# The first gate product of a DeltaNet/attention block, emitted with the last step of the scan

## The chip, the cores and the metric

The kernel runs on one core of one Trainium2 chip. The metric is the device time of one execution in microseconds (us), given as the median of several runs of the same program. A run is also taken with the hardware profiler; its rows are what this document reads. TensorE is called PE in them, VectorE DVE, ScalarE ACT, GpSimd POOL, and SP is the queue engine that issues most DMA transfers (ACT issues the rest).

## The reference, cut to what matters

One transformer-like layer on 1024 tokens of width 1024, all float32. The input projection's columns feed two groups of heads: a gated DeltaNet group (4 heads of 128, chunkwise with a state carried through the sequence) and a latent attention group (8 heads). Their outputs are joined, projected, normalised and added; a squared-ReLU MLP follows. The part that the change touches is the end of the DeltaNet group:

```python
    _, o = lax.scan(step, state0, xs)
...
    o = gated_delta_rule(q, k, v, beta, log_a)
    g = jax.nn.silu(gate.astype(jnp.float32)).reshape(bsz, s, GDN_HEADS, GDN_HEAD_DIM)
    o = rms_norm(o, out_norm) * g
...
        mixed = jnp.concatenate([o_gdn.astype(x.dtype), o_mla.astype(x.dtype)], axis=-1) @ w_out[l]
```

`gate` is one more 512-column slice of the input projection `h @ w_in`. So the gate of a head needs the normalised input and that head's 1024x128 block of the weight, and not the scan; only its product with the normalised scan output `o` does.

## The kernel before, in words

Every float32 matrix product that must be exact is done as three matmuls of split operands (`mm3`, lines 206 to 209): a high and a low part of each side. `stream` (L201) loads a 512 KB weight block into a `raw` buffer (three exist), and `split` (L196) makes the pair: a cast on ACT (L198, tile `whi`) and a subtraction on DVE (L199, tile `wlo`); three such pairs exist too. All such loads, and those of `load_head` and `gate`, go through `load_chained` (L182), which ties each to the one before: on SP they are issued in the order in which the program emitted them.

The work runs in stages. First come the normalisation, the projections and the preparation of the DeltaNet chunks. These are interleaved by `Weave`, a planner with costs written by hand. Then `scan()` (L861) goes through 8 chunks of 128 tokens and two more passes that drain it. It has its own PSUM pool, `psS`: four banks `pq` for the short products, two `po` for the outputs, two `ps`. In its pass c the outputs of chunk c-1 are finished (`outputs`, matmuls L916 and L917 into `ps_O`), normalised (`out_norm`, L921) and, one pass later, turned around by four transposes on PE, scaled on ACT and written to the DRAM tensor `d_go` (`out_rows`, L932, lines 937 to 939). `out_norm` is a chain: four squares with a sum on ACT (L927), one small operation on DVE (L928), a square root on ACT (L155), five small operations on DVE and the scaling of the whole tile (L930). Only then can the four transposes of that chunk start.

After the scan a new PSUM pool, `psB`, serves the attention. `units` lists 64 score blocks, a head and a block of 128 query rows each; for each the loop from L1185 on emits scores, softmax, transposes of the probabilities and the product with the values. Between them it emits pieces of `background()` (L1130): eight gate products `gate(h, half)` (L1092; a head and half of the tokens each, 24 matmuls in four pieces), then the DeltaNet part of the output projection. Ten pieces are emitted before the first score block, then about one with each.

A gate product needs PSUM bank `ou`, of which there is one; a Tanh on ACT (L1103), a combination on DVE that frees the bank (L1104), a product with the normalised scan output on POOL (L1105), and a write of the result to `d_gate` (L1106). Its scan output comes back from DRAM as tile `go` (two buffers), a load that must wait until the rows of `d_go` are written. `w_gate` holds the split weights of the four heads' gates: blocks 12 and 13 of the input weight are requested in passes 2 and 4 of the scan, block 14 after the first gate product and block 15 after the third.

A scheduler sets the order of instructions on each engine when the program is built, from the order of emission, the dependences and its own model of time; each engine then runs its list in that order, and an instruction that waits holds up all behind it on its engine.

Of the kernel before, what the change touches and what calls it, by code (L numbers as in the profile page):

```python
# [8 lines left out]
F32 = mybir.dt.float32  # L9
# [8 lines left out]
P = 128  # L18
# [86 lines left out]
def build(tc, a, out):  # L105
# [756 lines left out]
    def scan():  # L862
# [4 lines left out]
        for c in range(NT + 2):  # L867
            s = slice(c * P, (c + 1) * P)
            if c < NT:
                if c % 2 == 0:  # L870
                    yield f"load{c // 2}"
                if c in (2, 4):
                    w_gate.append(stream(a["w_qkvg"][11 + c // 2]))
# [29 lines left out]
            if 1 <= c <= NT:  # L903
                out_norm(c - 1)
            if c >= 2:
                out_rows(c - 2)
                if c % 2:
                    free("b", 3)
            yield step(5.0, 4.0, 3.0, lat=None)

    def outputs(c, heads):
# [57 lines left out]
    def load_values(h, lo):  # L969
        v = raw_tile()[:, :HALF].rearrange("p (b c) -> p b c", c=64)  # L970
        load_chained(v, d_v[:, :, h])
        e = h % 2
        V[h] = vt = vtile(f"V{h}").rearrange("p (b c) -> p b c", c=P)
        pair_of((vt[:, :, 64 * e : 64 * e + 64], vt[:, :, 64 - 64 * e : P - 64 * e]), v, lo)

    def filler():
# [114 lines left out]

    def gate(h, half):  # L1092
        s = slice(half * HALF, (half + 1) * HALF)
        o = lp.tile([P, HALF], F32, name="go", tag="go", bufs=2)
        load_chained(o, d_go[h, :, s])
        ps = psum("ps_gate", "ou")
        for k in range(KT):
            mm3(ps, cut(w_gate[h], slice(None), slice(k * P, (k + 1) * P)), h_cols(half, k), k == 0, k == KT - 1)
            if k % 2 and k < KT - 1:
                yield  # L1100

        g = lp.tile([P, HALF], F32, name="gate", tag="gate", bufs=2)
        nc.scalar.activation(g, ps, AF.Tanh, scale=0.5)  # L1103
        nc.vector.scalar_tensor_tensor(g, g, 1.0, ps, op0=ALU.add, op1=ALU.mult)  # L1104
        nc.gpsimd.tensor_tensor(g, g, o, op=ALU.mult)  # L1105
        nc.scalar.dma_start(d_gate[h, :, s], g)  # L1106
        yield

    def load_tokens(dst, src, j):
# [20 lines left out]
    def background():  # L1130
        for h, half in ((0, 0), (0, 1), (1, 0), (1, 1), (2, 0), (3, 0)):
            yield from gate(h, half)
            if h < 2 and half == 0:
                w_gate.append(stream(a["w_qkvg"][14 + h]))
            if (h, half) == (1, 1):
# [566 lines left out]
```

## Time and profile before

| what | value |
|---|---|
| median of 3 runs | 1280.64 us (1278.71 to 1283.99) |
| profiled execution | 1280.36 us |
| its span in the profile | 1278.6 us |
| PE busy | 1222.9 us (96% of the span) |
| DVE, ACT, POOL busy | 903.9, 651.9, 163.4 us |
| mean granted clock of PE | 0.985 |

The span lies inside the time of the execution; the 1.8 us between them are around the program's first and last instruction. In the rows of a timeline stand the start in us, the length in us, engine, line, operation, what it writes and reads, and in brackets how long the engine was idle before it and what ended that. A clock of 1.00 is PE's full speed.

### The profile page before, as it was taken

The page shows a single profiled execution, that of the slowest core. Times are in us where ns is not written, and L with a number is a line of the kernel's source. Part 1 is how long each engine was busy: PE and PEld are TensorE (multiplying, and loading weights), DVE is VectorE, ACT ScalarE, POOL GpSimd, SP SyncE. Part 2 cuts the span into 40 slices and gives each one's busy share as a digit, 9 for nine tenths or more (in the row PEclk, how much of TensorE's full clock was granted, in tenths as well). Part 3 has the DMA queues.
Part 4 walks back from the last instruction along what each step waited for, and adds up shares of the span by engine and source line. Part 5 has one row for each costly group of instructions (what it writes and reads, how often), then busy time and mean ns, then how long its engine had stood idle before and what let it go on. Part 6 is the DMA issues. An engine that isn't in the chain of part 4 may idle for free.

```text
span 1278.6 us, 17685 instructions
## 1 busy us (share of the span) xinstructions
PE 1222.9 (96%) x6224; PEld 1035.5 (81%) x6224; DVE 903.9 (71%) x1779; ACT 651.9 (51%) x1189; POOL 163.4 (13%) x152
## 2 busy tenths in 40 slices
PE   7999999999889999999898999999999999999995
PEld 6978888899778878887686888888887888888884
DVE  7678889546556785686976777677656786776744
ACT  6567643425645786774555544444445433344431
POOL 1011011220044553430000000000000000011021
PEclk9999999999989999999898999999999999999998
DMA  5114535736342511124444455455449984555902
GB/s 233 47 61 149 186 119 194 214 86 176 97 139 87 161 50 31 42 67 148 157 164 158 148 201 196 162 206 188 174 154 410 365 295 148 193 165 202 343 19 98
DMA packets 111217, 205.71 MB, mean 161 GB/s; under 512 B 33557, under 2 KB 51989, under 8 KB 111130
## 3 DMA queue, kind: packets, MB, share of 16 engines
q1 hardware_dynamic: 94848, 176.09, 41.1%
q10 hardware_dynamic: 16282, 28.50, 6.0%
q8 instruction: 49, 0.80, 0.3%
q14 instruction: 38, 0.31, 0.1%
HBM read 143.07 MB, written 61.49 MB: 160 GB/s over the span
## 4 chain that ended last, share of the span: by engine, by line
PE 60%; DVE 5%; DMA 3%; ACT 2%; issue 1%; POOL 1%; SPq 0%; DVEq 0%; ACTq 0%; POOLq 0%
PE ps_up L207 8%; PE ps_up L209 8%; PE ps_up L208 8%; PE ps_dn L208 8%; PE ps_dn L209 8%; PE ps_dn L207 8%; PE ps_PT L1061 2%; PE ps_out L207 2%; PE ps_out L208 1%; PE ps_out L209 1%; PE ps_o L1080 1%; PE ps_sc L207 1%; PE ps_o L1079 1%; PE ps_sc L208 1%; PE ps_sc L209 1%
## 5 line engine op out<-in xcount | busy, mean ns | idle before, releaser
L1573 POOL TENSOR_TENSOR rows<-rows,gpost 128x512 f32<-128x512 f32 x16 | 23.9, 1512 | 654.8 <-ACT junk L1570 654.8
L209 PE MATMUL ps_proj<-hThi,wlo 128*128 128x512 f32 x192 | 75.1, 395 | 1.2 <-DVE wlo L199 1.2
L207 PE MATMUL ps_proj<-hThi,whi 128*128 128x512 f32 x192 | 76.0, 396 | 0.0
L208 PE MATMUL ps_proj<-hTlo,whi 128*128 128x512 f32 x192 | 76.0, 396 | 0.0
L1065 DVE TENSOR_TENSOR PTlo<-ps_PT,PThi 128x512 fp32r<-128x512 f32 (+2 forms) x96 | 52.0, 550 | 20.0 <-ACT PThi L1064 19.3
L1064 ACT CAST PThi<-ps_PT 128x512 fp32r<-128x512 f32 (+2 forms) x96 | 45.4, 481 | 29.7 <-PE ps_PT L1061 28.1
L1505 DVE TENSOR_TENSOR dlo<-draw,dhi 128x1024 fp32r<-128x1024 f32 x35 | 44.7, 1301 | 22.0 <-ACT dhi L1504 21.9
L208 PE MATMUL ps_dn<-dlo,dhi 128*128 128x512 f32 x144 | 56.0, 389 | 0.0
L209 PE MATMUL ps_dn<-dhi,dlo 128*128 128x512 f32 x144 | 56.0, 389 | 0.0
L207 PE MATMUL ps_dn<-dhi 128*128 128x512 f32 x144 | 55.5, 389 | 0.0
L1325 ACT CAST whi<-raw 128x1024 fp32r<-128x1024 f32 (+1 forms) x29 | 26.3, 906 | 54.7 <-PE ps_up L208 48.9
L1035 ACT ACTIVATE Pt<-ps_sc,nm 128x896 f32<-128x896 f32 (+3 forms) x64 | 48.0, 749 | 11.8 <-DVE nm L1033 7.6
L1504 ACT CAST dhi<-draw 128x1024 fp32r<-128x1024 f32 x35 | 36.1, 1048 | 34.1 <-issue 13.8
L1061 PE MATMUL ps_PT<-ident,Pt 128*128 128x128 f32 x288 | 46.6, 276 | 2.4 <-DVE PTlo L1065 1.2
L1033 DVE TENSOR_REDUCE nm<-ps_sc 128x1 f32<-128x896 f32 (+3 forms) x64 | 47.8, 750 | 1.2
L1040 POOL TENSOR_TENSOR Pt<-Pt,rs 128x128 f32<-128x128 f32 (+4 forms) x40 | 35.4, 885 | 89.1 <-DVE rs L1038 65.1
L199 DVE TENSOR_TENSOR wlo<-raw,whi 128x1024 fp32r<-128x1024 f32 (+1 forms) x27 | 33.7, 1251 | 17.5 <-ACT whi L198 14.9
L1079 PE MATMUL ps_o<-PThi,V 128*128 128x256 f32 (+1 forms) x160 | 41.2, 280 | 3.2 <-DVE o L1086 1.4
L209 PEld LDWEIGHTS ps_proj<-hThi,wlo 128*128 128x128 f32 x192 | 36.1, 188 | 9.2 <-DVE wlo L199 1.7
L208 PEld LDWEIGHTS ps_proj<-hTlo,whi 128*128 128x128 f32 x192 | 36.1, 188 | 7.4 <-issue 0.5
L207 PEld LDWEIGHTS ps_proj<-hThi,whi 128*128 128x128 f32 x192 | 36.1, 188 | 7.4 <-issue 0.5
L1080 PE MATMUL ps_o<-PTlo,V 128*128 128x256 f32 (+1 forms) x160 | 41.2, 300 | 0.0
(589 smaller groups left out, 3969.6 us busy)
## 6 DMA issues: line engine op xcount, KB each, us to landing
draw<-in_w_down_dram SPq DMA_DIRECT2D x47, 512.0 KB
draw<-d_act SPq DMA_DIRECT2D x41, 512.0 KB
raw<-in_w_up_dram SPq DMA_DIRECT2D x40, 512.0 KB
raw<-in_w_down_dram SPq DMA_DIRECT2D x17, 512.0 KB
raw<-in_w_qkvg_dram SPq DMA_DIRECT2D x16, 512.0 KB
d_act<-c SPq DMA_DIRECT2D x16, 512.0 KB
d_act<-s SPq DMA_DIRECT2D x16, 512.0 KB
raw<-d_act SPq DMA_DIRECT2D x15, 512.0 KB
```

The lines of the kernel that those rows point to most:

```text
L207: mm(ps, lhs[0], rhs[0], start=start, stop=False, **kw)
L208: mm(ps, lhs[0], rhs[1], start=False, stop=False, **kw)
L209: mm(ps, lhs[1], rhs[0], start=False, stop=stop, **kw)
L1033: nc.vector.tensor_reduce(nm, ps[:, :npc, :w], axis=AX.XY, op=ALU.max, negate=True)
L1035: nc.scalar.activation(Pt[:, :n].rearrange("p (i w) -> p i w", i=npc), ps[:, :npc, :w], AF.Exp, bias=nm, scale=1.0, accum_out=sm)
L1061: transpose(ps[:, j * P : (j + 1) * P], Pt[:, b * P : (b + 1) * P], ident)
L1064: nc.scalar.copy(hi[:, :n, cs], ps3)
L1065: nc.vector.tensor_sub(lo[:, :n, cs], ps3, hi[:, :n, cs].bitcast(F32))
L1079: mm(ps[:, cs], V[h][:, b], hi[:, cs], start=(b == 0), stop=False)
L1080: mm(ps[:, cs], V[h][:, b], lo[:, cs], start=False, stop=(b == nb - 1))
L1504: nc.scalar.copy(hi, raw)
L1505: nc.vector.tensor_tensor(lo, raw, hi.bitcast(F32), op=ALU.subtract)
```

## The change

`gate` moves up, next to the scan, and can take its PSUM bank and its two tiles from other pools. The last pass of the scan (c = 9) starts `gate(0, 0)` with a bank of the scan's `pq` set and with tiles `hf` of the scan's memory, and emits three of its four pieces; the fourth follows after the pass. `background()` therefore has seven gate products left and begins with `gate(0, 1)`. The third gate's weight, block 14, is requested in pass 6 of the scan, as 12 and 13 are in passes 2 and 4; block 15 is still requested after `gate(1, 0)`. Lines of the scan after the new code are six higher than before: L917 is now L923, L927 is L933, L937 is L943, L939 is L945; the gate's Tanh is L994, its DVE and POOL operations L995 and L996, its write L997.

```diff
@@ -869,7 +869,7 @@
             if c < NT:
                 if c % 2 == 0:
                     yield f"load{c // 2}"
-                if c in (2, 4):
+                if c in (2, 4, 6):
                     w_gate.append(stream(a["w_qkvg"][11 + c // 2]))
                 kb = block(c)[0]
                 if c > 0:
@@ -902,11 +902,17 @@
                         )
             if 1 <= c <= NT:
                 out_norm(c - 1)
+            if c == NT + 1:
+
+                g = gate(0, 0, "pq", half_tile)
+                for _ in range(3):
+                    next(g)
             if c >= 2:
                 out_rows(c - 2)
                 if c % 2:
                     free("b", 3)
             yield step(5.0, 4.0, 3.0, lat=None)
+        next(g)
 
     def outputs(c, heads):
         _, pb, qb = block(c)
@@ -972,6 +978,24 @@
         e = h % 2
         V[h] = vt = vtile(f"V{h}").rearrange("p (b c) -> p b c", c=P)
         pair_of((vt[:, :, 64 * e : 64 * e + 64], vt[:, :, 64 - 64 * e : P - 64 * e]), v, lo)
+
+    def gate(h, half, tag="ou", tile=None):
+        s = slice(half * HALF, (half + 1) * HALF)
+        tile = tile or (lambda name: lp.tile([P, HALF], F32, name=name, tag=name, bufs=2))
+        o = tile("go")
+        load_chained(o, d_go[h, :, s])
+        ps = psum("ps_gate", tag)
+        for k in range(KT):
+            mm3(ps, cut(w_gate[h], slice(None), slice(k * P, (k + 1) * P)), h_cols(half, k), k == 0, k == KT - 1)
+            if k % 2 and k < KT - 1:
+                yield
+
+        g = tile("gate")
+        nc.scalar.activation(g, ps, AF.Tanh, scale=0.5)
+        nc.vector.scalar_tensor_tensor(g, g, 1.0, ps, op0=ALU.add, op1=ALU.mult)
+        nc.gpsimd.tensor_tensor(g, g, o, op=ALU.mult)
+        nc.scalar.dma_start(d_gate[h, :, s], g)
+        yield
 
     def filler():
         yield "v1"
@@ -1089,23 +1113,6 @@
                 mixT[p] = mtile(f"mixhi{p}"), mtile(f"mixlo{p}")
             pair_of(cut(mixT[p], slice(None), hs), oT[p][:, hs], nc.gpsimd)
 
-    def gate(h, half):
-        s = slice(half * HALF, (half + 1) * HALF)
-        o = lp.tile([P, HALF], F32, name="go", tag="go", bufs=2)
-        load_chained(o, d_go[h, :, s])
-        ps = psum("ps_gate", "ou")
-        for k in range(KT):
-            mm3(ps, cut(w_gate[h], slice(None), slice(k * P, (k + 1) * P)), h_cols(half, k), k == 0, k == KT - 1)
-            if k % 2 and k < KT - 1:
-                yield
-
-        g = lp.tile([P, HALF], F32, name="gate", tag="gate", bufs=2)
-        nc.scalar.activation(g, ps, AF.Tanh, scale=0.5)
-        nc.vector.scalar_tensor_tensor(g, g, 1.0, ps, op0=ALU.add, op1=ALU.mult)
-        nc.gpsimd.tensor_tensor(g, g, o, op=ALU.mult)
-        nc.scalar.dma_start(d_gate[h, :, s], g)
-        yield
-
     def load_tokens(dst, src, j):
         load_chained(dst.rearrange("p (h t) -> p h t", h=GH), src[:, :, 256 * j : 256 * (j + 1)].rearrange("h p t -> p h t"))
 
@@ -1128,10 +1135,10 @@
         return mtile("whi4"), mtile("wlo4")
 
     def background():
-        for h, half in ((0, 0), (0, 1), (1, 0), (1, 1), (2, 0), (3, 0)):
+        for h, half in ((0, 1), (1, 0), (1, 1), (2, 0), (3, 0)):
             yield from gate(h, half)
-            if h < 2 and half == 0:
-                w_gate.append(stream(a["w_qkvg"][14 + h]))
+            if (h, half) == (1, 0):
+                w_gate.append(stream(a["w_qkvg"][15]))
             if (h, half) == (1, 1):
                 w = [[stream(a["w_out"][0, 0])], []]
         load_gates((0,), raw_tile)
```

The next pieces show, word for word, where instructions stand in the lists of three engines.

ACT, end of the scan, before. `oj` is the square of a chunk's outputs (L927, "x2" two heads), `qb` the scaled transposes, `ro_t` the square root; `kT`, `qT` and `V` are the operands of the first attention head.

```order
L927 ACTIVATE oj,so<-ps_O 128x128 x2
L938 ACTIVATE qb_3247<-ps_onT,cols 128x512
L927 ACTIVATE oj,so<-ps_O 128x128
L939 DMA d_go<-qb_3247 128x4x128
L927 ACTIVATE oj,so<-ps_O 128x128
L155 ACTIVATE ro_t<-so 128x4
L943 CAST kT_3601<-raw 96x1024
L943 CAST qT_3603<-raw 96x1024
L943 CAST V_3617<-raw 128x8x64
L938 ACTIVATE qb_3247<-ps_onT,cols 128x512
L939 DMA d_go<-qb_3247 128x4x128
L198 CAST whi<-raw 128x1024
```

The same place on ACT after the change:

```order
L944 ACTIVATE qb_3247<-ps_onT,cols 128x512
L933 ACTIVATE oj,so<-ps_O 128x128
L994 ACT_TABLE_LOAD
L994 ACTIVATE gate<-ps_gate 128x512
L945 DMA d_go<-qb_3247 128x4x128
L933 ACTIVATE oj,so<-ps_O 128x128
L155 ACT_TABLE_LOAD
L155 ACTIVATE ro_t<-so 128x4
L997 DMA d_gate<-gate 128x512
L949 CAST kT_3639<-raw 96x1024
L944 ACTIVATE qb_3247<-ps_onT,cols 128x512
L949 CAST qT_3641<-raw 96x1024
```

The gate's Tanh now stands between the third and the fourth square of the last chunk, with a load of ACT's function table ahead of it and another one ahead of the square root. Before, the first Tanh stood behind the cast of a weight (`whi`), after the last chunk was done. Behind the rows shown come, after the change, the cast of `V`, the write of the last chunk to `d_go`, the cast of block 15's weight, a third table load and the Tanh of `gate(0, 1)`.

PE at the same place, before. `ps_O` with `vtok_2528` and `vtok_2957` are the last two heads' outputs of the last chunk, `ps_onT` the transposes, "x8" those of the last two chunks.

```order
L886 MATMUL ps_s_3510<-vtok_2957,Z_2773 128x128
L917 MATMUL ps_O<-vtok_2189,pb_3244 128x128
L916 MATMUL ps_O<-kb_3241,qb_3247 128x128
L917 MATMUL ps_O<-vtok_2528,pb_3244 128x128
L916 MATMUL ps_O<-kb_3241,qb_3247 128x128
L917 MATMUL ps_O<-vtok_2957,pb_3244 128x128
L937 MATMUL ps_onT<-ident,pb_3244 128x128 x8
L207 MATMUL ps_gate<-hThi_142,whi 128x512
```

PE after the change, from the last five of the eighteen gate matmuls that now stand ahead of the last two heads' outputs (two more stand ahead of `vtok_2189`):

```order
L207 MATMUL ps_gate<-hThi_144,whi 128x512
L208 MATMUL ps_gate<-hTlo_145,whi 128x512
L923 MATMUL ps_O<-vtok_2528,pb_3244 128x128
L922 MATMUL ps_O<-kb_3241,qb_3247 128x128
L923 MATMUL ps_O<-vtok_2957,pb_3244 128x128
L943 MATMUL ps_onT<-ident,pb_3244 128x128 x4
L209 MATMUL ps_gate<-hThi_144,wlo 128x512
L207 MATMUL ps_gate<-hThi_144,whi 128x512
L208 MATMUL ps_gate<-hTlo_145,whi 128x512
L209 MATMUL ps_gate<-hThi_144,wlo 128x512
L943 MATMUL ps_onT<-ident,pb_3244 128x128 x4
L207 MATMUL ps_gate<-hThi_146,whi 128x512
```

So 20 of the 24 matmuls of `gate(0, 0)` stand ahead of the last chunk's last outputs, four between the two groups of transposes, and `gate(0, 1)` (`hThi_146`) follows behind the last transposes. Behind it come the first two score blocks and then `gate(1, 0)`, which needs the one bank `ou` that `gate(0, 1)` holds.

SP behind the scan's own loads, before:

```order
L183 DMA go<-d_go 128x512
L183 DMA raw<-in_w_qkvg_dram 128x1024
L183 DMA go<-d_go 128x512 x2
L183 DMA raw<-d_k 64x1024
L183 DMA raw<-d_kr 32x1024
L183 DMA raw<-d_q 64x1024
L183 DMA raw<-d_r 32x1024
L183 DMA raw<-in_w_qkvg_dram 128x1024
```

SP after the change:

```order
L183 DMA go<-d_go 128x512
L183 DMA raw<-d_k 64x1024
L183 DMA raw<-d_kr 32x1024
L183 DMA raw<-d_q 64x1024
L183 DMA raw<-d_r 32x1024
L183 DMA raw<-d_v 128x8x64
L183 DMA go<-d_go 128x512 x2
L183 DMA raw<-in_w_qkvg_dram 128x1024
L183 DMA go<-d_go 128x512
L183 DMA raw<-d_k 64x1024
```

The first head's five loads, which before stood far ahead among the loads of the preparation, now stand behind the first `go`; block 14's load has gone up to their former place (with its cast and subtraction); and the next weight load, now block 15, stands behind two loads of `go`, the first of which reads the last chunk's rows of `d_go`. Before, the next weight load (block 14) stood ahead of that one.

## The prediction

> **What bounds the kernel now.** I read the page first, then the windows around the end of the scan, then the timelines of PE, ACT and SP there.
>
> ```profile
> PE 1222.9 (96%) x6224; PEld 1035.5 (81%) x6224; DVE 903.9 (71%) x1779; ACT 651.9 (51%) x1189; POOL 163.4 (13%) x152
> ```
>
> ```profile
> 338.00:344.00 6.00, 1.97 (x15) 1.73 (x14) 2.63 (x9) 4.54 (x13) 0.00 (x0) 0.87 0.27 81
> 356.00:362.00 6.00, 4.08 (x25) 3.45 (x23) 1.52 (x6) 2.47 (x4) 1.23 (x1) 1.00 0.93 280
> 362.00:372.00 10.00, 8.43 (x26) 7.09 (x27) 5.25 (x10) 4.18 (x11) 7.88 (x6) 0.66 0.38 102
> 382.00:424.00 42.00, 42.00 (x238) 36.55 (x237) 26.21 (x57) 23.90 (x50) 21.97 (x16) 1.00 0.34 99
> ```
>
> A window's row gives its bounds and length, the busy time of PE, PE's weight loads, DVE, ACT and POOL, then the granted clock, the DMA share and GB/s. PE bounds the kernel: it is busy for 96% of the span. So the change can move the time only by making PE idle, or run at a lower clock, for more or less time. It adds no matmul. PE has two holes in this stretch, at 338 to 344 and 356 to 372; from 382 to 424 it has none. Its timeline shows both:
>
> ```profile
> 336.66 0.61 PE L886 MATMUL ps_s<-vtok,Z 128*128 128x128 f32 x4
> 337.11 0.39 PE L917 MATMUL ps_O<-vtok,pb 128*128 128x128 f32 x2
> ...
> 337.77 0.49 PE L917 MATMUL ps_O<-vtok,pb 128*128 128x128 f32 x2
> ...
> 338.32 0.39 PE L917 MATMUL ps_O<-vtok,pb 128*128 128x128 f32 x2
> 338.54 0.60 PE L937 MATMUL ps_onT<-ident,pb 128*128 128x128 f32 x4
> 343.18 1.12 PE L937 MATMUL ps_onT<-ident,pb 128*128 128x128 f32 x4 [4.03 <-DVE pb L930]
> 343.94 0.78 PE L207 MATMUL ps_gate<-hThi,whi 128*128 128x512 f32 x1
> ...
> 350.42 0.37 PE L207 MATMUL ps_sc<-kT,qT 96*128 96x448 f32 x1
> ...
> 353.03 0.40 PE L207 MATMUL ps_gate<-hThi,whi 128*128 128x512 f32 x1
> ...
> 358.49 0.22 PE L207 MATMUL ps_sc<-kT,qT 96*128 96x128 f32 x1
> ...
> 359.81 0.28 PE L209 MATMUL ps_sc<-kT,qT 96*128 96x256 f32 x1
> 363.57 0.64 PE L207 MATMUL ps_sc<-kT,qT 96*128 96x320 f32 x1 [3.49 <-ACT Pt L1035]
> ...
> 365.34 0.63 PE L207 MATMUL ps_gate<-hThi,whi 128*128 128x512 f32 x1
> ...
> 372.94 1.04 PE L1061 MATMUL ps_PT<-ident,Pt 128*128 128x128 f32 x8
> ```
>
> First hole: PE has turned around chunk 6 (338.54) and waits 4.03 us for the normalisation of chunk 7. Second hole: 3.49 us for ACT. After each the clock is low for a while. The second gate product, undisturbed, takes 358.49 - 353.03 = 5.46 us, 0.2275 us for each of 24 matmuls. The first takes 350.42 - 343.94 = 6.48 us, 1.0 us more, and the four transposes before it 0.3 us more than those at 338.54 (0.76 to the next row against about 0.45). The third takes 372.94 - 365.34 = 7.60 us, 2.1 us more, and the six score matmuls before it 1.77 us, of which about half would go at full clock (an estimate from the matmul's 0.63 against 0.40 us). So the first hole costs 4.03 + 1.3 = 5.3 us, the second 3.49 + 2.1 + 0.9 = 6.5 us. These 11.8 us are all that can be won here.
>
> **The change part by part.** The edit that can win is the gate product in front of the first hole. The order of instructions shows what goes with it: on PE 20 of the 24 matmuls stand ahead of the last two heads' outputs of chunk 7, and on ACT the gate's Tanh stands between the third and the fourth square of that chunk. What that costs is read from ACT:
>
> ```profile
> 338.74 0.28 ACT L927 ACTIVATE oj<-ps_O 128x128 f32<-128x128 f32 x1 [0.77 <-PE ps_O L917]
> ...
> 340.13 0.21 ACT L927 ACTIVATION_READ_ACCUMULATOR oj<-ps_O 128x1 f32 x1
> ...
> 341.13 0.21 ACT L155 ACTIVATE ro_t<-so 128x4 f32<-128x4 f32 x1 [0.23 <-DVE so L928]
> ...
> 342.17 1.04 ACT L943 CAST qT<-raw 96x1024 fp32r<-96x1024 f32 x1
> 343.12 0.62 ACT L943 CAST V<-raw 128x512 fp32r<-128x512 f32 x1
> 344.33 0.69 ACT L938 ACTIVATE qb<-ps_onT,cols 128x512 f32<-128x512 f32 x1 [0.59 <-PE ps_onT L937]
> 345.05 0.37 ACTq L939 DMA_DIRECT2D d_go<-qb  x1
> ```
>
> ```profile
> 349.00 1.05 ACT L198 CAST whi<-raw 128x1024 fp32r<-128x1024 f32 x1 [3.98 <-DMA raw<-in_w_qkvg_dram]
> 350.07 1.28 ACT L1103 ACT_TABLE_LOAD   x1
> 351.36 0.60 ACT L1103 ACTIVATE gate<-ps_gate 128x512 f32<-128x512 f32 x1
> ```
>
> *Step 1, the squares start later.* They wait for the last outputs (0.77 us in the row). Before, those begin at 338.32. After, 20 matmuls of 0.2275 us, 4.55 us, lie in front, less the 0.3 us of gaps around 337.77 that they fill: 4.25 us later. First square: 338.74 + 4.25 = 343.0. PE ends the gate with the transposes of chunk 6 and four more matmuls at about 344.3, having lost nothing so far.
>
> *Step 2, ACT does the gate in the middle of the norm.* The third square's sum ends at 340.34 before, so 344.6 now. Then a table load, 1.28 us, to 345.87; the Tanh, 0.60 us, to 346.47 (its product is ready since 344.3); the fourth square, its sum about 0.3 us behind the Tanh, 346.75; a second table load, 1.28 us, to 348.05; the square root. From square root to transposes takes 343.18 - 341.13 = 2.05 us: 350.1. PE is idle from 344.3 to 350.1, 5.8 us where 4.03 us were. The gate product's 5.5 us are no longer behind the hole, but the hole is as far back as they were long, and a little wider.
>
> A table load shows 1.28 us in the row at 350.07, with 0.02 us between the cast's end and its start and 0.01 us to the Tanh. The Trainium skill, in "ScalarE: Activation LUTs", section "What ACT_TABLE_LOAD costs", gives about 1.28 us for the load and about 1.38 us more to drain the engine, 2.66 us for each switch, and its rule in "Table sets: the hidden batching unit" speaks against this change: do all calls of one set before the other. The load agrees with the trace, the drain is not seen in it; with the page's sum the two switches would cost 2.8 us more and the forecast would be 1287.8 us.
>
> *Step 3, PE up to its next wait.* Transposes at 350.1, 0.76 us at the low clock, then `gate(0, 1)`: 5.46 us and 1.0 to 2.1 us for the clock, then two score blocks, 353.03 - 350.42 = 2.6 us. PE is through at 359.9 to 361.0. Then comes `gate(1, 0)`, which needs bank `ou`; DVE frees it behind the Tanh of `gate(0, 1)`, and that Tanh stands on ACT behind the cast of block 15.
>
> ```profile
> 351.99 0.69 DVE L1104 SCALAR_TENSOR_TENSOR gate<-gate,ps_gate 128x512 f32<-128x512 f32 x1 [0.68 <-ACT gate L1103]
> ```
>
> ```profile
> 344.27 0.36 SPq L183 DMA_DIRECT2D raw<-in_w_qkvg_dram  x1
> 349.87 4.52 SPq L183 DMA_DIRECT2D go<-d_go  x2
> ```
>
> ```profile
> SPq L850 <- DMA d_go<-qb: 3.8, 1, 3.8
> ```
>
> ```profile
> 407.89 1.73 DMA go<-d_go
> 419.00 3.53 DMA raw<-in_w_out_dram
> ```
>
> *Step 4, when block 15 arrives.* It is queued on SP behind a `go` that waits for chunk 7's write to `d_go`. The scaled transposes start 344.33 - 343.18 = 1.15 us behind the transposes, at 351.25. ACT then casts `qT` (0.95 us from row to row) and `V` (0.62 us) before it issues the write: about 353.4. In the timeline of before SP issued that `go` 349.87 - 345.05 = 4.8 us behind the write's issue; another wait of SP for such a write lasted 3.8 us. So SP gets on at 357.2 to 358.2, issues two `go` (0.9 us with the gaps, from issues of 0.36 us) and asks for block 15 at 358.1 to 359.1. The like load took 349.00 - 344.27 = 4.7 us, a load of the same size 3.5 us at 419: cast at 361.6 to 363.8. Cast, table load, Tanh and DVE take 352.68 - 349.00 = 3.7 us: bank free at 365.3 to 367.5. I take 367, near the same kind of load. PE, idle since about 360.5, has lost 6.5 us where the second hole had 3.49.
>
> *Step 5, the sum.* I count from 367: `gate(1, 0)` 5.46 us; the low clock after the hole, 1.3 to 3.0 us by the two holes of before, which do not order by their length, 2.0 us taken; what before was done by 372.94 and now is not, two small score blocks and seven transposes (358.49 to 360.09 there, 1.6 us) and a score block of 0.9 us. That gives 377.0 against 372.94, 4.0 us later; bounds 365.3 with 1.3 us and 367.5 with 3.0 us, 1.6 and 5.5 us. `gate(1, 1)` can wait again for ACT, which casts the second head's operands first: their loads are also behind the `go` loads on SP; some 0.4 us, as PE has the 1.6 us of small work in between. Together +4.4 us.
>
> *The rest costs nothing that I can see.* Block 14's cast and subtraction move up into the preparation, where ACT has room:
>
> ```profile
> 273.70 0.59 ACT L823 COPY Yl<-ps_Y 128x512 f32<-128x512 f32 x1 [9.34 <-PE ps_Y L817]
> ```
>
> ACT idles 9.34 us there, waiting for PE; without that cover it would be 1.05 us on ACT (the `whi` cast's row) and as long again on DVE.
>
> ```profile
> 335.10 0.34 SPq L183 DMA_DIRECT2D go<-d_go  x1
> ```
>
> ```profile
> 352.76 1.28 POOL L1105 TENSOR_TENSOR gate<-gate,go 128x512 f32<-128x512 f32 x1 [66.25 <-DVE gate L1104]
> ```
>
> The first head's five loads move behind the first `go` on SP. Even if that were issued no earlier than before, at 335.10, they would have 13 us until their first cast. The gate's write (L997) now stands ahead of that cast on ACT and waits for POOL until about 348.5 (the Tanh's end at 346.47, 0.69 us on DVE, 1.28 us on POOL). Nothing behind it is due before the transposes at 350.1, so this wait is covered by the norm.
>
> ```profile
> 426.97 0.35 PE L1079 MATMUL ps_o<-PThi,V 128*128 128x256 f32 x1 [1.14 <-DVE o L1086]
> ```
>
> Further on the pieces of `background()` come about four score blocks earlier and so end earlier. Small waits like this one of 1.14 us will move; I allow 2 us either way and take none.
>
> **The rivals.** (a) *The gate fills the first hole.* If the norm of chunk 7 did not wait for the Tanh, the transposes would start at 344.3, and 5.3 us would be won. For it: the gate needs nothing of the scan. Against it: ACT's order. And the second hole stays: chunk 7's write at about 347.5, block 15 asked for at 353.2, bank free at 361.7 instead of 367, and the sum is 1.3 us below before: 1279.3 us. Only if block 15 came early too would both holes go, 11.8 us, 1269 us.
>
> (b) *Slower: block 15 is held up by the transfers ahead of it.* Two `go` of 256 KB are issued just before it. If it had to wait for both (1.73 us each in the row at 407.89), the bank would be free at 370.5 instead of 367: 1288.5 us. Over 0.5% is reached when `gate(1, 0)` starts after 369.0. For it: the window 356 to 362 moves 280 GB/s while the second head's operands come late (DMA share 0.93). Against it: block 14 took 4.7 us although a `d_go` write ran beside it.
>
> (c) *A table load waits for the engine to run empty.* It would wait for the operation ahead of it, at most a cast's 1.05 us a load, 2.1 us for the two: 1287.1 us. The 0.02 us in front of the load speak against it; this is the mechanism of the page on activation tables.
>
> (d) *It evens out.* The later holes around 427 close because PE's work arrives in another order: 1281 us.
>
> **How the numbers follow.** Forecast as summed, +4.4 us: 0.56. (a) 0.12, of that 0.03 for 1269; (b) 0.18; (c) 0.04; (d) 0.10. Set against the profiled execution's 1280.36 us the sum is 1284.8 us; the median of before lies 0.3 us above that execution, so for the median 1285.0 us. The bounds of the sum, +1.6 to +5.9 us with the 2 us of the later waits on both sides, give 1280 to 1288.5; (b) reaches to 1290 and (a) to 1278. 0.5%, about what a measurement of this kernel can tell from no change, is 6.4 us: 1274.2 to 1287.0. Faster than that: 0.04, both holes gone. Slower: (b), (c) and the upper end of the forecast, 0.22. The rest, 0.74, is no change.
>
> **What would show it.** In the profile after: PE idle of 5 to 6 us ahead of the last four `ps_onT` (L943) instead of 4.03; two table loads on ACT between the third square and the square root; a wait of ACT's `whi` cast for `raw<-in_w_qkvg_dram` ending about 363, and PE idle of 5 to 7 us ahead of the gate product behind two score blocks; the product `gate(1, 0)` starting at 365 to 368. Step 2 is wrong if the last transposes start before 347; step 4 if PE does not idle ahead of `gate(1, 0)`; both wrong makes it faster. If both holes are as said and the time is still that of before, the loss was given back later, between 380 and 630.

## The result, and the profile after

| | before | after |
|---|---|---|
| median of the runs of this comparison | 1279.97 us | 1295.70 us (1294.27 to 1296.78) |
| profiled execution, its span | 1280.36, 1278.6 us | 1296.78, 1295.0 us |

The changed kernel is slower: the ratio after to before is 1.0114, with a 95% interval of 1.0096 to 1.0133, some 12 to 17 us. The prediction had 1285.0 us and a range of 1278 to 1290, and gave 0.74 to no change: it was wrong.

By the profile page after, PE does the same number of matmuls as before and is busy 8.4 us longer with them, as it is where the granted clock is lower (its mean is 0.979, 0.985 before):

```profile
PE 1231.3 (95%) x6224; PEld 1040.5 (80%) x6224; DVE 903.9 (70%) x1779; ACT 655.2 (51%) x1191; POOL 163.1 (13%) x152
```

First the place that the prediction worked out. ACT's timeline after, at the end of the scan (L933 the squares, L994 the gate's Tanh, L155 the square root, L945 the write of the last chunk, L198 block 15's cast):

```profile
343.94 0.28 ACT L933 ACTIVATE oj<-ps_O 128x128 f32<-128x128 f32 x1 [5.03 <-PE ps_O L923]
...
345.56 1.28 ACT L994 ACT_TABLE_LOAD   x1
346.86 0.60 ACT L994 ACTIVATE gate<-ps_gate 128x512 f32<-128x512 f32 x1
...
347.73 1.28 ACT L155 ACT_TABLE_LOAD   x1
349.02 0.20 ACT L155 ACTIVATE ro_t<-so 128x4 f32<-128x4 f32 x1
...
352.94 0.37 ACTq L945 DMA_DIRECT2D d_go<-qb  x1
...
360.73 1.05 ACT L198 CAST whi<-raw 128x1024 fp32r<-128x1024 f32 x1 [6.37 <-DMA raw<-in_w_qkvg_dram]
```

SP's timeline between that write and that cast:

```profile
355.26 0.82 SPq L183 DMA_DIRECT2D go<-d_go  x2
356.19 0.36 SPq L183 DMA_DIRECT2D raw<-in_w_qkvg_dram  x1
```

PE's timeline after. Its first three waits of this stretch, and then five of those that were not forecast:

```profile
351.07 1.11 PE L943 MATMUL ps_onT<-ident,pb 128*128 128x128 f32 x4 [5.81 <-DVE pb L936]
...
364.52 0.50 PE L207 MATMUL ps_gate<-hThi,whi 128*128 128x512 f32 x1 [1.85 <-DVE gate L995]
...
373.62 0.50 PE L207 MATMUL ps_gate<-hThi,whi 128*128 128x512 f32 x1 [1.93 <-DVE gate L995]
...
433.42 0.33 PE L207 MATMUL ps_sc<-kT,qT 96*128 96x128 f32 x1 [2.32 <-ACT Pt L1059]
...
436.12 0.80 PE L207 MATMUL ps_out<-whi,ghi 128*128 128x512 f32 x1 [1.22 <-ACT part L1169]
...
488.13 0.35 PE L1103 MATMUL ps_o<-PThi,V 128*128 128x256 f32 x1 [1.24 <-ACT part L1169]
...
557.66 0.44 PE L207 MATMUL ps_sc<-kT,qT 96*128 96x384 f32 x1 [0.93 <-ACT Pt L1059]
...
561.37 0.30 PE L1085 MATMUL ps_PT<-ident,Pt 128*128 128x128 f32 x1 [1.41 <-DVE PTlo L1089]
```

The hole ahead of the last transposes is 5.81 us, the 5.8 us of the prediction. The second hole, 3.49 us before, is two smaller ones of 1.85 and 1.93 us. Of the five waits below them four are longer than any that the trace of before has from 380 to 600 us, where the longest is the 1.14 us at 426.97.

To see where, the two traces are laid side by side at the same piece of work: the addition on DVE that closes the last output of attention head 0, and the one that closes that of head 7, the last. Before:

```profile
406.94 0.42 DVE L1086 TENSOR_TENSOR o<-ps_o,th 64x256 f32<-64x256 f32 x1
...
587.84 0.43 DVE L1086 TENSOR_TENSOR o<-ps_o,th 64x256 f32<-64x256 f32 x1 [0.27 <-ACT th L1085]
```

After:

```profile
416.45 0.40 DVE L1110 TENSOR_TENSOR o<-ps_o,th 64x256 f32<-64x256 f32 x1
...
603.04 0.43 DVE L1110 TENSOR_TENSOR o<-ps_o,th 64x256 f32<-64x256 f32 x1 [0.17 <-ACT th L1109]
```

At head 0's end the changed kernel is 9.51 us late. But it has emitted the same number of background pieces by then *besides* the gate product that it did in the scan, so it is four pieces, one gate product of 5.46 us, further on. Its true lag is 9.51 - 5.46 = 4.05 us. At head 7's end all pieces are done in both and the lag is 15.20 us. So 11.15 us are lost between these two marks, and 1.2 us behind them (the spans differ by 16.4).

The windows between the marks, cut once more where the last background matmul ends (549.60 before, 553.10 after). Columns as in the prediction: PE's busy time is the second number, the granted clock the last but two. Before:

```profile
406.94:549.60 142.66, 137.15 (x810) 119.28 (x809) 101.03 (x233) 101.04 (x219) 67.67 (x56) 0.99 0.27 80
549.60:587.84 38.24, 35.98 (x227) 31.12 (x226) 27.97 (x68) 23.93 (x61) 8.17 (x10) 1.00 0.11 34
```

After:

```profile
416.45:553.10 136.65, 126.96 (x744) 110.11 (x744) 95.51 (x220) 93.69 (x202) 61.35 (x50) 0.98 0.24 68
553.10:603.04 49.94, 44.80 (x267) 39.46 (x266) 34.07 (x81) 30.15 (x76) 13.38 (x15) 0.93 0.08 28
```

The second row of each pair is attention without background work: 38 us before, 50 us after, with 40 more of the attention's own matmuls left to do alone. PE idles 5.14 us there instead of 2.26, at a clock of 0.93 instead of 1.00 (7% of 44.8 us, some 3 us): about 6 us. In the first rows PE idles 9.69 us instead of 5.51, at a clock 0.01 lower (1.3 us): 5.5 us. Together 11.5 us, near the 11.15 of the marks.

### The profile page after: what moved, and what is told of

It is laid out like the page before. It is cut to its first block, busy times and chain, and to the rows that moved or that the text cites. A ratio compares the mean times of both kernels' runs of the same rounds, so it can differ in the third digit from the quotient of the medians.

```text
span 1295.0 us, 17705 instructions
## 1 busy us (share of the span) xinstructions
PE 1231.3 (95%) x6224; PEld 1040.5 (80%) x6224; DVE 903.9 (70%) x1779; ACT 655.2 (51%) x1191; POOL 163.1 (13%) x152
## 4 chain that ended last, share of the span: by engine, by line
PE 60%; DVE 6%; ACT 3%; DMA 3%; issue 1%; SPq 0%; POOL 0%; DVEq 0%; ACTq 0%
PE ps_up L207 8%; PE ps_up L209 8%; PE ps_up L208 8%; PE ps_dn L208 8%; PE ps_dn L209 8%; PE ps_dn L207 7%; PE ps_PT L1085 2%; PE ps_out L207 1%; PE ps_out L209 1%; PE ps_out L208 1%; PE ps_o L1104 1%; PE ps_o L1103 1%; PE ps_sc L207 1%; PE ps_gate L207 1%; PE ps_sc L208 1%
## 5 line engine op out<-in xcount | busy, mean ns | idle before, releaser
L1088 ACT CAST PThi<-ps_PT 128x512 fp32r<-128x512 f32 (+2 forms) x96 | 44.8, 480 | 33.5 <-PE ps_PT L1085 32.6
L1085 PEld LDWEIGHTS ps_PT<-ident,Pt 128*128 128x128 f32 x288 | 34.6, 142 | 9.8 <-issue 2.9
```

Source lines behind the costliest of these rows:

```text
L1085: transpose(ps[:, j * P : (j + 1) * P], Pt[:, b * P : (b + 1) * P], ident)
L1088: nc.scalar.copy(hi[:, :n, cs], ps3)
```

## The experiments

Three theories stood after this look. *Pace*: the four pieces that `background()` has fewer, with the pace of the loop unchanged, put every later piece four score blocks early. Heavier work meets another part of a head, and the pieces run out four blocks earlier than before. *Start*: what happens from 280 to 380 us (block 14 in the scan, the table loads, the wait for block 15) delays all that follows. *Order*: the scheduler's lists fall out differently after any edit, with no cause to be named. The loop's pace, on which many runs differ, is this condition (L1186 before):

```python
while bg and emitted < (10 + i * 23 / 24 if i < 24 else 33 + (i - 24) * 32 / 33):
```

### The two halves of the change

Only the weight's request (`e1_weight`), in the kernel before:

```diff
-                if c in (2, 4):
+                if c in (2, 4, 6):
...
-            if h < 2 and half == 0:
-                w_gate.append(stream(a["w_qkvg"][14 + h]))
+            if (h, half) == (1, 0):
+                w_gate.append(stream(a["w_qkvg"][15]))
```

> The kernel before with only the weight's request moved to the scan's sixth step; the gate products stay where they were. Theory 'pace': pieces and pace are untouched, so only the 0.94 us that the changed kernel is late at 281 us, and a shorter or longer wait for the third gate's cast: 1280 to 1282. Theory 'start', in the form that the request's loads and casts in the scan are what hurts: 1286 to 1296.

Measured: 1280.36 us, ratio 1.0001 (0.9990 to 1.0012). The request costs nothing and wins nothing.

Only the gate product (`e2_gate`): the changed kernel without `6` in that tuple, and with `w_gate.append(stream(a["w_qkvg"][14]))` ahead of the first piece of `background()`.

> The changed kernel with the weight's request back outside the scan, as the first thing of the background work; the gate product stays with the scan's last step. Theory 'pace': the four pieces still run ahead, so 1292 to 1296, less the 0.94 us at 281 us. Theory 'start' in the form 'the request in the scan': 1281 to 1284.

Measured: 1296.40 us, 1.0121 (1.0104 to 1.0138), 0.4 us above the upper end of what *pace* gave, and far from *start*. The whole loss belongs to the moved gate product. *Start* in the form of block 14 falls.

### The pace

In the changed kernel the pace is counted from 4 (`e3_pace`):

```diff
-    bg, emitted = background(), 0
+    bg, emitted = background(), 4
```

> The changed kernel, with the pace of the background work counted from 4 instead of 0, so that each piece after the moved gate is emitted at the score block at which it stood before the change. Theory 'pace' (the 10 to 12 us lost between 390 and 620 us come from later pieces emitted four score blocks too early, and running out four blocks too early): the attention's lag behind the kernel before stays at the 3 to 4 us that it has at 390, so about 1283.5 us (1282 to 1286). Theory 'start' (what happens between 280 and 380 us, the wait for block 15, the table loads and the block-14 preparation, is what delays all that follows): no change, 1294 to 1297. Theory 'order' (the scheduler's list falls out differently wherever an input changes): anything between 1283 and 1300, with no reason for the former.

Measured: 1292.56 us, 1.0106 (1.0077 to 1.0134). *Pace* expected 1283.5: a miss. In the trace the loss between the marks is gone for the most part, 2.9 us are left of 11.15. But only six pieces stand ahead of the first score block now, where the changed kernel has ten, and PE waits longer for the Tanh behind block 15:

```profile
366.55 0.80 PE L207 MATMUL ps_gate<-hThi,whi 128*128 128x512 f32 x1 [4.79 <-DVE gate L995]
```

So this run mends one thing and harms another; the runs below keep the ten. By the marks the harm is small, a lag of 4.4 us at the first one against 4.1. The profiled execution is the fastest of four that took 1290.08 to 1297.39 us, and the run's interval covers the changed kernel's ratio, so why so little came back stays open.

The pace alone, in the kernel before, whose first gate product is where it was (`e7_before_early`):

```diff
-        while bg and emitted < (10 + i * 23 / 24 if i < 24 else 33 + (i - 24) * 32 / 33):
+        while bg and emitted < (14 + i * 23 / 24 if i < 24 else 37 + (i - 24) * 32 / 33):
```

> The kernel before, untouched but for its pace: every background piece is allowed four pieces earlier (14 and 37 in the place of 10 and 33). The first gate product is where it was. Theory 'pace': PE is idle more behind 420 us, as in the changed kernel, and the time goes up by 8 to 12 us, to 1288 to 1292. Theories 'start' and 'order': the two holes at 350 and 372 us are untouched, so 1280 within 3 us.

Measured: 1290.68 us, 1.0079 (1.0059 to 1.0098). The kernel before is made some 10 us slower with nothing but earlier pieces; *start* and *order* expected none of that. Two of its holes are those of the changed kernel to within 0.01 us, 1.24 us at 488.13 and 1.41 us at 561.37 there:

```profile
482.85 0.36 PE L1079 MATMUL ps_o<-PThi,V 128*128 128x256 f32 x1 [1.24 <-ACT part L1162]
...
557.91 0.30 PE L1061 MATMUL ps_PT<-ident,Pt 128*128 128x128 f32 x1 [1.40 <-DVE PTlo L1065]
```

The changed kernel with only the later part of the pace put back, from block 24 (`e8_late`), and with only the end of it, from block 40 (`e14_end`):

```diff
-(10 + i * 23 / 24 if i < 24 else 33 + (i - 24) * 32 / 33)
+(10 + i * 23 / 24 if i < 24 else 29 + (i - 24) * 32 / 33)
```

```diff
-(10 + i * 23 / 24 if i < 24 else 33 + (i - 24) * 32 / 33)
+(10 + i * 23 / 24 if i < 24 else (33 if i < 40 else 29) + (i - 24) * 32 / 33)
```

> The changed kernel, with only the later part of the pace put back: from the 24th score block on each piece comes where it was (29 in the place of 33), before that four blocks early as in the changed kernel. This splits the loss of 'pace': if it is the later pieces that run out too early, the idle time behind 450 us falls from 12.1 to some 8 or 9 us and the time to 1289 to 1293, while the 3.8 us of idle time at 433 to 436 stays. If it is the early half (pieces that wait for gates and loads at 420 to 440), 1294 to 1297.

> The changed kernel with only the last of the pace put back: up to the 39th score block each piece comes four blocks early as in the changed kernel, from the 40th on none comes until the kernel before is caught up with, so that the pieces end with the same score block as before the change and not four blocks ahead. If most of what the later half of the pace is worth (5.5 us in the run that puts the pace back from the 24th block) is the running out, the holes of 557 to 572 us (0.93, 1.40, 0.46 and 0.71 us) and the granted clock of 0.83 at 560 to 580 us go, and the time is 1289 to 1292. If it lies at blocks 24 to 40, where the holes of 485 to 488 us stay, 1294 to 1297.

Measured: 1290.19 us, 1.0080 (1.0057 to 1.0103), and 1292.62 us, 1.0090 (1.0061 to 1.0118). The first is as *pace* had it, 5.5 us off the changed kernel's time; the second, 0.6 us above its range, is 3 us off. So the running out is about half of what the later part is worth, by medians whose intervals overlap.

The changed kernel with its ten pieces at the start, then none until the kernel before is caught up with at the fifth block (`e12_start`):

```diff
-(10 + i * 23 / 24 if i < 24 else 33 + (i - 24) * 32 / 33)
+(max(10, 6 + i * 23 / 24) if i < 24 else 29 + (i - 24) * 32 / 33)
```

> The changed kernel with the ten pieces ahead of the first score block as they are, and no further piece until the kernel before is caught up with, so that from the fifth score block on each piece stands where it stood before the change. Theory 'pace' with the forecast's sum for the tail (4.4 us): the tail's loss stays and what is lost between 407 and 588 us falls from 11.4 us (aligned at the attention's evictions, with the four pieces' 5.7 us taken off) to the 1 to 3 us of the runs with the pace put back: 1284 to 1288. If it matters when in the first 24 blocks the pieces are late, nothing better than the 1290 of the run that puts only the later half back.

Measured: 1287.80 us, 1.0051 (1.0034 to 1.0069), in the expected range. Its windows between the marks, cut where the last background matmul ends, are again those of before, 38.64 us without background work against 38.24:

```profile
411.56:553.73 142.17, 134.66 (x798) 117.07 (x797) 103.44 (x234) 101.32 (x219) 65.84 (x56) 0.99 0.24 72
553.73:592.37 38.64, 35.77 (x228) 31.30 (x227) 28.11 (x70) 24.68 (x62) 8.15 (x10) 1.00 0.11 36
```

The lag is 4.62 us at the first mark and 4.53 us at the second. This is the decisive run: the same change, the same edit of the scan's end, with half of the loss gone.

### The end of the scan

The moved gate's Tanh held behind the square root (`e4_tanh`); `after(x, y)` makes instruction x wait for y, and `root` is that square root, set for this one gate product alone:

```diff
-        nc.scalar.activation(g, ps, AF.Tanh, scale=0.5)
+        tanh = nc.scalar.activation(g, ps, AF.Tanh, scale=0.5).ins
+        if root:
+            after(tanh, root[0], "the last norm goes first")
```

> The changed kernel, with the moved gate's Tanh held behind the last norm's square root, so that no table is loaded between the last squares and that root. The hole ahead of the last transposes falls by the load and the Tanh, 1.28 + 0.60 us, from 5.81 to about 3.9 us. Theory 'pace': that is all of it, and the rest of the loss stays: 1293 to 1295. Theory 'start' in the form that ACT's table loads in the scan's tail throw the later order over: 1281 to 1285.

Measured: 1296.39 us, 1.0133 (1.0106 to 1.0160). The 2 us did not come. No table is loaded between the squares and the root any more, but the hole is 6.30 us. The wait moved to DVE; its timeline shows the gate's combination (L1000) between two steps of the norm, waiting 1.53 us for the Tanh, and behind it a step of the norm (L165) that took 1.26 us, where the same step before took 0.17 us (the last section comes back to it):

```profile
347.52 0.16 DVE L163 TENSOR_TENSOR ro_t<-ro 128x4 f32<-128x4 f32 x1
349.22 0.69 DVE L1000 SCALAR_TENSOR_TENSOR gate<-gate,ps_gate 128x512 f32<-128x512 f32 x1 [1.53 <-ACT gate L997]
349.82 0.15 DVE L164 TENSOR_TENSOR ro_t<-ro_t,so 128x4 f32<-128x4 f32 x1
350.01 1.26 DVE L165 TENSOR_SCALAR ro_t<-ro_t 128x4 f32<-128x4 f32 x1
```

So the run does not test what it was made for, the price of the table loads.

With the Tanh held, the gate's first matmul held behind the scan's last output (`last_out`) as well (`e5_both`):

```diff
+            if root and k == 0:
+                after(first, last_out[0], "the last outputs go first")
```

> As the run with the held Tanh, and the moved gate's first matmul held behind the scan's last output, so that the gate's matmuls stand in the hole behind the scan (some 16 at 0.24 us) instead of ahead of the last outputs. The hole ahead of the last transposes falls from 5.81 to under 1 us; the wait for block 15 ahead of gate(1,0), 1.85 us, may grow by 1 to 2. Theory 'pace': 3 to 5 us come back here and the losses behind 420 us stay, 1290 to 1293. Theory 'start': with the tail mended all of it comes back, 1279 to 1283.

Measured: 1284.92 us, 1.0036 (1.0023 to 1.0049): 10 us less than the changed kernel, where 3 to 5 were expected. The hole ahead of the last transposes is gone (none of over 0.3 us), and with it the low clock behind it, which the expectation left out. The window of 340 to 380 us had 30.41 us of PE work at a clock of 0.87 in the changed kernel; here:

```profile
340.00:380.00 40.00, 38.51 (x197) 32.26 (x196) 20.83 (x44) 21.26 (x44) 13.29 (x10) 1.00 0.45 137
```

At the first mark this kernel is 7.2 us *ahead* of the kernel before, and between the marks it loses 9.5 us, much as the changed kernel does (11.2); PE's wait for ACT is even longer at the like place (2.32 us at 433.42 in the changed kernel):

```profile
422.21 0.33 PE L209 MATMUL ps_sc<-kT,qT 96*128 96x128 f32 x1 [2.82 <-ACT Pt L1069]
```

Both together, with the pace counted from 4 (`e6_both_pace`):

> Both mends together: the moved gate held behind the scan's last output, its Tanh behind the root, and the pace counted from 4. Theory 'pace' with the forecast's sum for the tail: the two losses add, so 3 to 5 us under the run with the pace alone (1292.6), that is 1287 to 1290; where the mended pace brings its full 8 us as in its profiled execution, 1281 to 1285, hardly under the kernel before. If the hole behind the scan is truly filled and nothing is late next, 1276 to 1279, under both kernels.

Measured: 1281.36 us, 1.0013 (0.9997 to 1.0029): the kernel before, not under it. Six pieces at the start are too few again: its lead at the first mark is 1.6 us, not 7.2.

### Versions that might beat both kernels

The gate held as above, with the pace of the decisive run (`e9_both_start`), and the kernel before with 14 pieces at the start and its own pace behind (`e11_before_start`):

```diff
-(10 + i * 23 / 24 if i < 24 else 33 + (i - 24) * 32 / 33)
+(max(14, 10 + i * 23 / 24) if i < 24 else 33 + (i - 24) * 32 / 33)
```

> The run with the gate held behind the scan's last output, which was 7.4 us ahead of the kernel before at 407 us, with the pace of the run above: ten pieces ahead of the first score block, then none until the kernel before is caught up with. Theory 'pace': the lead stays and 1 to 3 us are lost behind it, 1273 to 1277, under both kernels. If the four pieces at the start were not what made the lead, as with the pace counted from 4 throughout: 1280 to 1283.

> The kernel before with 14 pieces ahead of the first score block in the place of 10, and no further piece until its own pace has caught up. The first gate is not moved. Theory 'pace' (early pieces help while the start waits, and cost where they run out): in the run with the whole pace earlier the start was 5.4 us ahead at 407 us and 15.6 us were lost behind it; here the lead stays and 0 to 2 us are lost, 1275 to 1278, under the kernel before. If the cost comes with any shift of the pieces: 1288 to 1292.

Measured: 1279.13 us, 0.9992 (0.9980 to 1.0005), and 1278.68 us, 0.9990 (0.9978 to 1.0002). Both miss their ranges, by 2.1 and 0.7 us, and neither is shown to be faster than the kernel before. The leads at the first mark are there, 7.2 and 5.6 us, but 4.3 and 2.4 us are lost again between the marks. In the first of the two PE idles 7.2 us from 378 to 450 us, where the kernel before idles 1.7.

### All runs side by side

Lag (+) or lead (-) against the trace of before at the first mark, with 5.46 us taken off where four pieces more are done; what is lost from there to the second mark; PE's idle time and clock between the marks. These are one profiled execution each, and it lies up to 2.7 us from the median of its kernel, so differences of up to some 3 us mean little here. Each ratio is taken against runs of the kernel before that were made beside it; their medians are 1279.90 to 1281.02 us.

| kernel | ratio | first mark | lost between | PE idle, clock |
|---|---|---|---|---|
| before | 1 | 0 | 0 | 7.8, 0.99 |
| pieces four blocks early throughout | | | | |
| changed | 1.0114 | +4.1 | 11.2 | 14.8, 0.96 |
| gate alone (`e2_gate`) | 1.0121 | +5.7 | 9.6 | 14.9, 0.97 |
| Tanh held (`e4_tanh`) | 1.0133 | +4.6 | 10.0 | 14.3, 0.96 |
| gate held (`e5_both`) | 1.0036 | -7.2 | 9.5 | 15.5, 0.97 |
| before, early pace (`e7_before_early`) | 1.0079 | -5.1 | 15.3 | 15.9, 0.97 |
| the same, but put back later | | | | |
| put back from block 40 (`e14_end`) | 1.0090 | +2.1 | 6.3 | 13.3, 0.98 |
| put back from block 24 (`e8_late`) | 1.0080 | +3.7 | 5.1 | 11.3, 0.97 |
| put back from block 5 or earlier | | | | |
| `e12_start` | 1.0051 | +4.6 | -0.1 | 10.4, 0.99 |
| `e3_pace` | 1.0106 | +4.4 | 2.9 | 11.1, 1.00 |
| `e6_both_pace` | 1.0013 | -1.6 | 0.9 | 10.2, 0.98 |
| `e9_both_start` | 0.9992 | -7.2 | 4.3 | 11.1, 0.98 |
| `e11_before_start` | 0.9990 | -5.6 | 2.4 | 8.4, 1.00 |

Whatever the scan's end looks like, pieces that are early throughout cost 9.5 to 15 us between the marks, and pieces in their old places 0 to 4. What follows the second mark is not in the table: by the spans the kernels with an edit lose 0 to 4 us more there (the changed kernel 1.2, the decisive run 2.9), which no run was made for and whose cause stays open.

## Why the prediction was wrong

**Step 1** was right: the first square is at 343.94, 343.0 forecast; the 0.9 us between them is there ahead of the scan already, and the run with the early pace of the kernel before, which is the same program up to the scan's end, ends its first hole at 343.92, where the kernel before did at 343.18: two executions differ by as much.

**Step 2** was right to the tenth: two loads of 1.28 us and the Tanh between squares and root, 5.81 us of idle time. Of the further 1.38 us for each switch that the Trainium skill, in "ScalarE: Activation LUTs", section "What ACT_TABLE_LOAD costs", adds for a drain, nothing shows: the first load ends at 346.84, the Tanh starts at 346.86, the second ends at 349.01, the root starts at 349.02. Step 3 was too low on the low clock behind that hole: `gate(0, 1)` took from 351.84 to 359.89, 8.05 us, 2.6 us over its time at full clock, where 1.0 to 2.1 were allowed.

**Step 4** had the mechanism and not the size. Block 15 does wait behind a `go` that waits for the last chunk's write. But that write was issued at 352.94, when the scaled transposes that it writes were done, and ahead of the cast of `V` (353.74), which stands before it in ACT's list and by the prediction held it up. And SP issued that `go` 2.3 us behind the write (352.94 to 355.26), not 3.8 to 4.8; block 15 took 4.5 us, and `gate(1, 0)` began at 364.52, not 367, after 1.85 us of idle time instead of 6.5. The wait of `gate(1, 1)`, 0.4 us in step 5, was 1.93.

**Step 5**, the sum of 4.4 us, was near, with 4.05 us at the first mark, but by luck: its terms were off and made up for each other. At 371.69, ahead of the wait of `gate(1, 1)`, PE had all done that the kernel before had by 372.94 but for the score block of 0.9 us, so it was some 0.3 us ahead, where the sum had 4.0 us of lag. `gate(1, 0)` took 5.57 us (364.52 to 370.09), so the 2.0 us of low clock that step 5 put there did not come. Then `gate(1, 1)` waited 1.93 us and took 7.18 us (373.62 to 380.80), 1.7 us over 5.46, where the sum had 0.4 us for the wait and nothing for the clock. And 0.9 us of the 4.05 were there ahead of the scan (step 1). The decisive run, with this loss and without the other, is 4.4 to 8.8 us over the kernel before by its interval, and 4.5 us late at the second mark.

**The step that failed** is the last part, "The rest costs nothing that I can see", with the sentence "Further on the pieces of `background()` come about four score blocks earlier and so end earlier. Small waits like this one of 1.14 us will move; I allow 2 us either way and take none." The fact was seen and its price was taken from one small wait. It is 11.15 us by the marks and 8 us by the medians with and without it (1295.7 and 1287.8). Of the other items of that part, block 14 in the scan did cost nothing (`e1_weight`, 1.0001). The reasons, as far as the traces show them: in the attention without background work PE idles 2.26 us in 38 us before and 5.14 us in 50 us after, at a clock of 1.00 and of 0.93, so the four blocks from which the pieces are missing cost idle time and then clock; and the casts that come with the pieces meet other score blocks. ACT's timeline in the changed kernel at the hole of 433.42, where a cast waits for its load with the softmax of a 896-wide block queued behind it:

```profile
430.67 1.04 ACT L198 CAST whi<-raw 128x1024 fp32r<-128x1024 f32 x1 [1.89 <-DMA raw<-in_w_out_dram]
431.62 0.74 ACT L1088 CAST PThi<-ps_PT 128x512 fp32r<-128x512 f32 x2
432.25 1.02 ACT L1059 ACTIVATE Pt<-ps_sc,nm 128x896 f32<-128x896 f32 x1
```

Before, the like cast waited for nothing, and the softmax ahead of it was 128 wide:

```profile
430.06 0.40 ACT L1035 ACTIVATE Pt<-ps_sc,nm 128x128 f32<-128x128 f32 x1
...
430.41 1.07 ACT L198 CAST whi<-raw 128x1024 fp32r<-128x1024 f32 x1
```

Shown by runs is that the pieces' places cost this time; that this cast is the cause of that hole is read from the trace, and no run tried it alone. Nor is this hole what the decisive run mends: there the like cast waits 0.86 us for its load (at 429.48), and PE's longest wait of that stretch is no shorter:

```profile
431.31 0.52 PE L1085 MATMUL ps_PT<-ident,Pt 128*128 128x128 f32 x3 [2.84 <-DVE PTlo L1089]
```

By its windows it has both parts of the loss back, the 6 us without background work and the 5.5 us ahead of it, although PE idles 7.51 us ahead of it, against 9.69 in the changed kernel and 5.51 before. Which pieces cost those 5.5 us, and by which waits, stays open.

The prediction's closing sentence names the place, 380 to 630 us, but for the opposite case, a loss that is given back there.

**The rivals.** (a), the gate filling the first hole, did not happen, and `e5_both` made it happen: it is 7.2 us ahead at the first mark, where (a) had 1.3 us with the second hole left and 11.8 us without it, and the time is still 1284.9 us because the early pieces take that back. (b) did not come: block 15 took 4.5 us. (c): as under step 2. (d), that later holes close, had the sign wrong; larger ones came. That later holes could grow by *more* than 2 us was not among the rivals, and for the bound of 2 us the prediction shows one wait of 1.14 us.

## What to carry to other kernels

Work that is taken out of a paced stream of filler moves everything behind it: put the pace right in the same edit, or count what runs out at the end, from a stretch of the profile that has no filler. Where to put it right matters too: counting from 4 at the start (`e3_pace`) brought back 3 us by the medians and not clear of noise, keeping the ten pieces at the start and pausing behind them (`e12_start`) 8. A move that fills one hole is worth little when the same work was filling another one: count the filler, as the time is what PE idles in all and the clock at which it runs. And, as in `e4_tanh`, an instruction held back on one engine can move the wait to the engine that reads its result, when that engine's list has the urgent work behind it.

## What was not expected of the hardware

The granted clock fell after a short hole. After 9 us in which PE idled 0.3 us, then the 0.83 us below and 0.35 us more, at least two microseconds ran at half clock; windows and timeline of the changed kernel:

```profile
467.00:469.00 2.00, 2.00 (x11) 2.00 (x11) 1.58 (x6) 0.84 (x3) 0.00 (x0) 0.50 0.00 0
```

```profile
465.65 0.36 PE L1103 MATMUL ps_o<-PThi,V 128*128 128x256 f32 x1 [0.83 <-DVE ps_sc L1055]
466.35 0.86 PE L1085 MATMUL ps_PT<-ident,Pt 128*128 128x128 f32 x3 [0.35 <-DVE PTlo L1089]
```

The same two holes in the kernel before were followed by a clock of 1.00:

```profile
454.56 0.36 PE L1079 MATMUL ps_o<-PThi,V 128*128 128x256 f32 x1 [0.83 <-DVE ps_sc L1031]
455.26 0.52 PE L1061 MATMUL ps_PT<-ident,Pt 128*128 128x128 f32 x3 [0.35 <-DVE PTlo L1065]
```

```profile
455.00:460.00 5.00, 4.74 (x36) 4.57 (x37) 4.88 (x15) 3.52 (x10) 0.82 (x2) 1.00 0.11 33
```

The Trainium skill, in "TensorE: Matmul & The Clock Gate", section "What's actually happening", has the clock fall after an idle window of about 3.4 us, with windows that run free of the program. That the same hole is punished in one execution and not in another fits windows that run free; that 1.5 us of idle time in 11 us were enough does not fit an idle window of 3.4 us, if that means a window in which PE does nothing at all.

A DVE operation on 128x4 numbers took 1.26 us in the run with the held Tanh (350.01, above), against 0.17 us for the same operation in the kernel before (341.97). POOL's product of the gate started 0.03 us ahead of it there, and it ended 0.03 us behind that product:

```profile
349.98 1.26 POOL L1001 TENSOR_TENSOR gate<-gate,go 128x512 f32<-128x512 f32 x1 [61.77 <-DVE ro_t L164]
```

The Trainium skill, in "SBUF — State Buffer", section "SBUF: two separate sides", describes a port pair that DVE and GpSimd share and that goes as an exclusive lock to whichever operation starts first; on DVE's side it names operations in a 2-port mode or with two SBUF inputs. These two rows agree with it, though the trace does not show the mode of the DVE operation. In the changed kernel no such row stands in the norm.
